# DeltaNet decay rows copied by DMA instead of selector products, and the first loads re-ordered, in a two-layer hybrid trunk

## The chip, the cores and the metric

The kernel runs on one core of one Trainium2 chip. The metric is device time in microseconds (us) of one execution; before the change the median of three runs is 1322.48 us (1322.01 to 1324.29).

## What is computed

Two layers of a decoder trunk run over 272 tokens (16 meta tokens and 256 real ones) with 1024 channels. Each layer is half a SwiGLU feed-forward, a mixer, and half a SwiGLU again, each behind an RMSNorm. The mixer projects the normalised input once and splits it among four branches; the change touches the third, a chunked gated DeltaNet with 4 heads. Cut to what matters:

```
for l in range(DEPTH):
    h = h + 0.5 * swiglu(rmsnorm(h, ln_ffn1[l]), ffn1_wi[l], ffn1_wo[l])
    u = rmsnorm(h, ln_mix[l])
    h = h + hybrid_mixer(u, ...)
    h = h + 0.5 * swiglu(rmsnorm(h, ln_ffn2[l]), ffn2_wi[l], ffn2_wo[l])
y = rmsnorm(h, ln_final)
...
# DeltaNet branch
g = -exp(a_log) * softplus(p_a + dt_bias)
G = cumsum(g)
decay = exp(where(incl, G[:, None] - G[None, :], NEG_INF))
m = eye + where(strict, (kb @ k.T) * decay, 0)
qk = where(incl, (q @ k.T) * decay, 0)
```

So the decays are, for each head, a square over (earlier token, later token): the running sum G of the later token, less that of the earlier one, masked to the causal half, through exp.

## The kernel before, in words

Activations lie transposed, 128 channels to a partition block and 272 tokens along the row. Weights come as fp32 tiles `wf` of up to 1 MB on SyncE's DMA queue; ScalarE (ACT) writes the rounded part `wh` (L210) and VectorE (DVE) the rest `wl` (L184), and TensorE (PE) makes three products `j` for each weight tile, `xh,wh`, `xl,wh` and `xh,wl`. The activations are split likewise into `xh` and `xl`.

The program builds its own order. Every piece of work is a generator with a modelled time (`Chain`), a modelled clock stands for each engine, and a poller emits whichever step the model has ready first; buffers come from small pools ("S" and "L" are row buffers in SBUF, "px" is PSUM). What is emitted is a fixed order for each engine, and each engine runs its own strictly in order. A changed step therefore shifts its neighbours on every engine. Steps on GpSimd (POOL) go through `POOL` (L493), most memsets are emitted where their tile is taken.

The change touches two places. **The head**, `begin` (L729): x comes in four quarters of two tiles `xn`, the meta tokens in `mt`, the first two weight tiles in quarters too, all at once on SyncE's and ACT's queues. `setup` (L464) loads the first norm's gains (`g1r`) and turns them into columns (`g1p`). `columns(q)` transposes a quarter on PE (`xT`), `group(q)` makes `xh`, `xl`, `wh`, `wl` for two k-blocks and the squares for the norm (`scr`), and `before(k)` calls them between the products. **The decays**, `fab` (L1768): the running sums of all heads are three scans into rows 32 to 43 of `pk`, and those of DeltaNet's four heads are rows 36 to 39. Later, for each head, PE spreads one row over all partitions with a selector and adds a mask, and ACT takes the exp from PSUM with the bias `ns` (the earlier token's sum, negated):

```
self.mm(c, ps[:, :T], self.sel[:, h, :], pk[:, :T], True, False)
self.mm(c, ps[:, :T], self.identb, self.maskk, False, True)
```

`setup2` (L559) builds `sel` and `maskk` on POOL and DVE. Behind the running sums, `fab` also sends four rows of the forgetting attention from POOL's queue into `ka`, one for a head.

Of the kernel before, what the change touches and what calls it, by code (L numbers as in the profile page):

```python
# [8 lines left out]
F32 = mybir.dt.float32  # L9
F32R = mybir.dt.float32r  # L10
BF16 = mybir.dt.bfloat16
AF = mybir.ActivationFunctionType
# [3 lines left out]
P = 128  # L16
# [55 lines left out]
class Prog:  # L72
# [391 lines left out]
    def setup(self):  # L464

        nc, i = self.nc, self.i
        c = Chain("setup")
        self.ident = self.const([P, P], F32, "ident")
        self.ones = self.const([P, P], F32, "ones")
        nc.gpsimd.memset(self.ones, 1.0)  # L470
        nc.gpsimd.affine_select(out=self.ident, in_=self.ones, pattern=[[1, P]], compare_op=ALU.is_equal,
                                fill=0.0, base=0, channel_multiplier=-1)
        self.eps = self.const([P, 1], F32, "eps")
        nc.gpsimd.memset(self.eps, EPS)
        self.g1 = self.const([P, L * KD], F32, "g1")
        self.warm(7)
        rows = self.take("S", [L * KD, P], name="g1r")
        nc.scalar.dma_start(out=rows.ap, in_=i["ln_ffn1"].rearrange("l (k p) -> (l k) p", p=P))
        ps = self.take("px", name="g1p")
        c.t = 3500.0  # L480
        self.tr(c, ps[:, :L * KD], rows.ap)
        self.give(rows, c.t)
        self.V(c, "tensor_copy", out=self.g1, in_=ps[:, :L * KD])
        self.give(ps, c.t)
# [74 lines left out]
    def setup2(self, c):  # L559
# [16 lines left out]
        self.maskk = self.const([P, T], BF16, "maskk")  # L576
# [7 lines left out]
        mg = mf  # L584
        yield "pool"
        self.POOL(c, "memset", mg, 0.0)
        yield "pool"
        self.POOL(c, "affine_select", out=mg, in_=mg, pattern=[[1, P]], compare_op=ALU.is_ge,
                                fill=NEG, base=0, channel_multiplier=-1)
        yield "dve"  # L590
        self.V(c, "tensor_copy", out=self.maskk[:, 0:NM], in_=mg[:, 0:NM])
        for b in range(2):
            yield "dve"
            self.V(c, "tensor_copy", out=self.maskk[:, NM + b * P:NM + (b + 1) * P], in_=mg)
# [4 lines left out]
        misc = self.const([P, 768], F32, "sel")  # L599
        sel = misc[:, 0:512].rearrange("p (h c) -> p h c", h=4)  # L600
        o4 = self.ones[:, 0:1].to_broadcast([P, 4 * P]).rearrange("p (h c) -> p h c", h=4)
        yield "pool"
        self.POOL(c, "affine_select", out=sel, in_=o4, pattern=[[-1, 4], [0, P]], compare_op=ALU.is_equal,
                                fill=0.0, base=-36, channel_multiplier=1)
        self.sel = sel
# [22 lines left out]
        sel2 = misc[:, 512:768].rearrange("p (a c) -> p a c", a=2)  # L628
        yield "pool"
        self.POOL(c, "affine_select", out=misc[:, 512:768].rearrange("p (h c) -> p h c", h=4),  # L630
# [98 lines left out]
    def begin(self):  # L729
# [3 lines left out]
        nc.gpsimd.memset(mt.ap, 0.0)  # L733
# [5 lines left out]
        nc.scalar.dma_start(out=mt[0:NM], in_=i["meta"])  # L739
        wfs = [self.wpool.tile([P, 2048], F32, tag=f"wf{x}", name=self.name("wf")) for x in range(2)]  # L740
        for q in range(4):
# [3 lines left out]
            for x in range(2):  # L745
                nc.sync.dma_start(
                    out=wfs[x].rearrange("p (k c) -> p k c", k=KD)[:, 2 * q:2 * q + 2, :],
                    in_=self.chunks[x]["segs"][0][0][2 * q * P:2 * (q + 1) * P].rearrange("(k p) c -> p k c", p=P))
            self.staged[0], self.staged[1] = wfs
        self.nc_ = 2  # L750
        self.tab(AF.Sqrt)
        self.setup()
# [11 lines left out]
        scr = self.take("L", [P, D], name="scr")  # L764

        def columns(q):

            for k in (2 * q, 2 * q + 1):
                c = Chain("x", 3700.0 + 3000 * q)
# [7 lines left out]
        def group(q):  # L777
# [4 lines left out]
            for x, (k, ps, c) in enumerate(now):  # L782
# [6 lines left out]
                wc.t = max(wc.t, 4700.0 + 3000 * q + 1000 * x)  # L789
# [13 lines left out]
            for b in range(2):  # L803
                self.A(Chain("sq"), scr[:, 0:256], xn[b][:, q * 256:q * 256 + 256], AF.Square,
                       accum_out=ss[:, 4 * b + q:4 * b + q + 1])
            if q == 0:
# [4 lines left out]
        def factors(c):  # L811
# [3 lines left out]
            for r in xn + [mt, scr]:  # L815
                self.give(r, self.clk["act"])
# [23 lines left out]
        def before(k):  # L840
# [8 lines left out]
            if k == 3:  # L849
                columns(2)  # L850
                group(2)
            if k == 5:
                columns(3)
                group(3)
                self.LOOK = 0
# [912 lines left out]
    def fab(self, c):  # L1768
# [29 lines left out]
        for a, n in TOK:  # L1798
            yield "dve"
            self.V(c, "tensor_tensor_scan", out=pk[g, a:a + n], data0=self.ones[q, 0:1].to_broadcast([12, n]),  # L1800
                   data1=lg[q, a:a + n], initial=0.0, op0=ALU.mult, op1=ALU.add)
        yield AF.Exp
# [39 lines left out]

        dec = yield from self.take_wait(c, "L", [P, 4, T], name="dec")
        for h in range(4):
            ps = yield from self.take_wait(c, "px", name="dc")
            yield "pe"
            self.mm(c, ps[:, :T], self.sel[:, h, :], pk[:, :T], True, False)
            self.mm(c, ps[:, :T], self.identb, self.maskk, False, True)
            for ti, (a, n) in enumerate(TOK):
                yield AF.Exp  # L1850
                self.A(c, dec[:n, h, a:a + n], ps[:n, a:a + n], AF.Exp,
                       bias=ns[:n, ti * 64 + 16 + h:ti * 64 + 17 + h])
            self.give(ps, c.t)
        for x in st:
            self.give(x, c.t)
        self.dec = dec
# [471 lines left out]
```

## Time and profile before

| | before |
|---|---|
| median of 3 runs, us | 1322.48 |
| the profiled execution, us | 1322.03 |
| its span, us | 1320.3 |
| mean granted TensorE clock | 0.999 |
| PE busy | 99% |
| DVE busy | 66% |
| ACT busy | 54% |
| POOL busy | 15% |
| mean DMA rate | 163 GB/s |

Everything in the span is counted from its start. A timeline row gives the start, the length, the engine and the operation, and in brackets the engine's idle time ahead of it and who ended it. PE's matmuls overlap: a 128x272 product starts about 0.125 us after the one before it although its own row says 0.29, so the cost of a product is read between starts. Layer 0's mixer lies at some 215 to 410 us, layer 1's at some 875 to 1040 us.

### The profile page before, as it was taken

The numbers are of one execution on the slowest core, as the hardware profiler recorded it, in microseconds if no ns is written. First come the engines' busy times: TensorE is split into PE (matmuls) and PEld (weight loads), VectorE is DVE, ScalarE is ACT, GpSimd is POOL, SyncE is SP. The second block draws the span as 40 slices with busy tenths as digits, with TensorE's granted clock in tenths as the row PEclk, the third lists the DMA queues.
The fourth block names the chain that finished last, engine by engine and source line by source line (L and its number), as shares of the span: only waits on it lengthen the run. The fifth ranks groups of instructions, "written<-read, shape, count | busy, mean of one in ns | idle before, by whom it ended". The sixth has DMA issues, their size and how long they took to land.

```text
span 1320.3 us, 25744 instructions
## 1 busy us (share of the span) xinstructions
PE 1301.8 (99%) x10515; PEld 1267.7 (96%) x10515; DVE 876.6 (66%) x1521; ACT 718.5 (54%) x1156; POOL 192.5 (15%) x314
## 2 busy tenths in 40 slices
PE   8999999999999999999999999999999999999998
PEld 8999999999999999999999999999899999999986
DVE  4766556778767876565566565568796778766653
ACT  6445445896544564445454444459865545544542
POOL 1444001100004141110011110011000132111100
PEclk9999999999999999999999999999999999999999
DMA  7656555342333665555555555555333366555561
GB/s 225 195 184 198 176 170 165 111 160 91 118 111 128 202 205 162 190 162 175 176 183 169 182 169 176 172 149 157 100 111 111 117 197 199 192 190 178 197 201 48
DMA packets 210918, 214.62 MB, mean 163 GB/s; under 512 B 13324, under 2 KB 200048, under 8 KB 210800
## 3 DMA queue, kind: packets, MB, share of 16 engines
q1 hardware_dynamic: 208608, 210.62, 49.6%
q0 software_dynamic: 2128, 2.29, 0.7%
q8 instruction: 83, 1.36, 0.4%
q14 instruction: 35, 0.29, 0.1%
q10 hardware_dynamic: 64, 0.07, 0.0%
HBM read 211.90 MB, written 1.05 MB: 161 GB/s over the span
## 4 chain that ended last, share of the span: by engine, by line
PE 86%; ACT 7%; DVE 4%; issue 1%; DMA 1%; POOL 1%; SPq 0%; ACTq 0%; DVEq 0%; POOLq 0%
PE j L235 54%; PE o L235 15%; PE fo L235 5%; PE wo L235 4%; PE br L235 3%; ACT wh L210 2%; ACT L205 2%; DVE wl L184 1%; PE sc L235 1%; PE pv L235 1%; ACT sq L210 1%; DMA wf<-in_ffn_wi_dram 1%; PE pt L247 0%; PE p L235 0%; PE ku L235 0%
## 5 line engine op out<-in xcount | busy, mean ns | idle before, releaser
L235 PE MATMUL j<-xh,wh 128*128 128x272 f32 (+2 forms) x2224 | 647.9, 291 | 0.0
L235 PE MATMUL j<-xh,wl 128*128 128x272 f32 (+2 forms) x2224 | 636.6, 286 | 1.3 <-DVE wl L184 1.3
L235 PE MATMUL j<-xl,wh 128*128 128x272 f32 (+2 forms) x2224 | 635.5, 286 | 0.0
L184 DVE TENSOR_TENSOR wl<-wf,wh 128x1024 fp32r<-128x1024 f32 (+1 forms) x408 | 484.3, 1212 | 183.1 <-ACT wh L210 181.8
L210 ACT ACTIVATE wh<-wf 128x1024 fp32r<-128x1024 f32 (+1 forms) x408 | 408.0, 1027 | 104.4 <-PE o L235 73.0
L235 PEld LDWEIGHTS j<-xh,wh 128*128 128x128 f32 (+1 forms) x2224 | 418.0, 188 | 3.6 <-issue 0.3
L235 PEld LDWEIGHTS j<-xh,wl 128*128 128x128 f32 (+1 forms) x2224 | 418.5, 188 | 2.6 <-DVE wl L184 2.5
L235 PEld LDWEIGHTS j<-xl,wh 128*128 128x128 f32 (+1 forms) x2224 | 418.8, 188 | 0.8
L235 PE MATMUL o<-act,wh 128*128 128x272 f32 x1056 | 199.0, 288 | 0.0
L235 PEld LDWEIGHTS o<-act,wh 128*128 128x128 f32 x1056 | 165.8, 188 | 0.0
L235 PE MATMUL o<-act,wl 128*128 128x272 f32 x528 | 152.2, 288 | 0.0
L197 POOL TENSOR_TENSOR g<-g,R 128x272 f32<-128x272 f32 (+1 forms) x88 | 70.1, 797 | 415.6 <-ACT g L210 415.6
L210 ACT ACTIVATE act<-g 128x272 fp32r<-128x272 f32 (+1 forms) x88 | 37.7, 428 | 133.4 <-DVE g L184 133.4
L210 ACT ACTIVATE g<-g 128x272 f32<-128x272 f32 (+1 forms) x88 | 37.6, 428 | 124.8 <-DVE g L184 124.5
L235 PEld LDWEIGHTS o<-act,wl 128*128 128x128 f32 x528 | 99.4, 188 | 0.0
L184 DVE TENSOR_TENSOR g<-j,g 128x272 f32<-128x272 f32 (+1 forms) x88 | 38.1, 433 | 56.3 <-PE j L235 44.4
L210 ACT ACTIVATE gt<-gt,pv 128x272 f32<-128x272 f32 (+1 forms) x64 | 30.6, 511 | 72.2 <-DVE gt L184 70.9
L184 DVE TENSOR_TENSOR act<-g,act 128x272 fp32r<-128x272 f32 (+1 forms) x88 | 39.2, 446 | 40.4 <-ACT act L210 40.4
L197 POOL TENSOR_TENSOR sq<-sq,sq 128x272 f32<-128x272 f32 (+1 forms) x30 | 24.3, 811 | 240.0 <-ACT sq L210 226.5
L205 ACT ACT_TABLE_LOAD x43 | 55.2, 1283 | 2.9 <-POOL ones L470 2.2
L235 PE MATMUL fo<-wh,act 128*128 128x512 f32 x176 | 55.3, 395 | 0.0
L184 DVE TENSOR_TENSOR g<-j,R 128x272 f32<-128x272 f32 (+1 forms) x88 | 37.9, 432 | 12.1 <-PE j L235 11.7
(356 smaller groups left out, 1330.3 us busy)
## 6 DMA issues: line engine op xcount, KB each, us to landing
wf<-in_ffn_wi_dram SPq DMA_DIRECT2D x86, 1024.0 KB, 5.1
wf<-in_ffn_wo_dram SPq DMA_DIRECT2D x34, 1024.0 KB, 5.1
wf<-in_w_gate_dram SPq DMA_DIRECT2D x32, 1024.0 KB, 5.1
wf<-in_w_in_dram SPq DMA_DIRECT2D x16, 1024.0 KB, 5.2
wf<-in_ffn_wo_dram SPq DMA_DIRECT2D x12, 768.0 KB, 4.5
wf<-in_w_branch_dram SPq DMA_DIRECT2D x16, 512.0 KB, 3.5
wf<-in_w_out_dram SPq DMA_DIRECT2D x8, 1024.0 KB, 5.2
wf<-in_ffn_wi_dram SPq DMA_DIRECT2D x8, 256.0 KB, 4.4
```

The source lines that it names most:

```text
L184: getattr(self.nc.vector, op_)(**kw)
L197: getattr(self.nc.gpsimd, op_)(**kw)
L205: self.nc.scalar.preload_act_table_set(SETS[ok[0]])
L210: self.nc.scalar.activation(out=out, in_=in_, func=func, **kw)
L235: self.nc.tensor.matmul(out, lhsT, rhs, start=start, stop=stop)
```

## The change

In `fab`, right behind the three scans, four DMAs on POOL's queue copy rows 36 to 39 of `pk` (272 numbers, 1088 bytes each) to all 128 partitions of `dec`, one DMA for a head, so 128 pieces of 1088 bytes in each and 512 pieces (557 KB) in a layer. Three affine_selects on POOL then mask `dec` in place, and ACT's exps read and write `dec` in SBUF instead of reading PSUM. The selector, its mask and the PE products for them are gone. In the head, ACT's queue starts with `g1r` and the first quarter of one weight tile, `mt` follows them; the memset of `mt` goes from POOL to DVE, half of the squares from ACT to DVE, and the third and fourth quarter of x are transposed one k-block earlier.

```
@@ fab
+        dec = yield from self.take_wait(c, "L", [P, 4, T], name="dec")
+        d = Chain("dec", c.t)
+        yield "pool"
+        for h in range(4):
+            self.POOL(d, "dma_start", out=dec[:, h, :], in_=pk[36 + h:37 + h, None, :T].to_broadcast([1, P, T]))
+        d.t += 3000
+        for a, n in TOK:
+            self.POOL(d, "affine_select", out=dec[:n, :, a:a + n], in_=dec[:n, :, a:a + n], pattern=[[0, 4], [1, n]],
+                      compare_op=ALU.is_ge, fill=NEG, base=0, channel_multiplier=-1)
+            d.t += 4 * n * 2.0
+        self.dec_t = d.t
...
-        dec = yield from self.take_wait(c, "L", [P, 4, T], name="dec")
-        for h in range(4):
-            ps = yield from self.take_wait(c, "px", name="dc")
-            yield "pe"
-            self.mm(c, ps[:, :T], self.sel[:, h, :], pk[:, :T], True, False)
-            self.mm(c, ps[:, :T], self.identb, self.maskk, False, True)
-            for ti, (a, n) in enumerate(TOK):
-                yield AF.Exp
-                self.A(c, dec[:n, h, a:a + n], ps[:n, a:a + n], AF.Exp,
-                       bias=ns[:n, ti * 64 + 16 + h:ti * 64 + 17 + h])
-            self.give(ps, c.t)
+        c.t = max(c.t, self.dec_t)
+        for ti, (a, n) in enumerate(TOK):
+            for h in range(4):
+                yield AF.Exp
+                self.A(c, dec[:n, h, a:a + n], dec[:n, h, a:a + n], AF.Exp,
+                       bias=ns[:n, ti * 64 + 16 + h:ti * 64 + 17 + h])
@@ begin
-        nc.gpsimd.memset(mt.ap, 0.0)
+        rows = self.take("S", [L * KD, P], name="g1r")
+        nc.scalar.dma_start(out=rows.ap, in_=i["ln_ffn1"].rearrange("l (k p) -> (l k) p", p=P))
+        nc.vector.memset(mt.ap, 0.0)
...
-        nc.scalar.dma_start(out=mt[0:NM], in_=i["meta"])
...
-                nc.sync.dma_start(
+                eng = nc.sync if q or x else nc.scalar
+                eng.dma_start(
...
+            if q == 0:
+                nc.scalar.dma_start(out=mt[0:NM], in_=i["meta"])
...
-            if k == 3:
+            if k == 2:
                 columns(2)
                 group(2)
-            if k == 5:
+            if k == 4:
                 columns(3)
                 group(3)
+            if k == 5:
```

In all, PE loses the 8 `dc` visits (two products each), and ACT's table loads go from 43 to 51: four more among the first layer's setup, two fewer in layer 0's mixer, and six more in layer 1's.

The first place is the head of ACT's order. Before (`mt` meta tokens, `g1r` gains, `xh` and `wh` the split input and weights, `scr` squares):

```order
L739 DMA mt_71<-in_meta_dram 16x1024
L205 ACT_TABLE_LOAD
L478 DMA g1r_132<-in_ln_ffn_dram 16x128
L210 ACTIVATE xh_81<-xT_151,g_9_123 128x272
L210 ACTIVATE wh_137<-wf_98 128x512
L210 ACTIVATE xh_82<-xT_155,g_9_123 128x272
L210 ACTIVATE wh_141<-wf_99 128x512
```

and now:

```order
L714 DMA g1r_72<-in_ln_ffn_dram 16x128
L728 DMA wf_99<-in_ffn_wi_dram 128x2x256
L732 DMA mt_71<-in_meta_dram 16x1024
L205 ACT_TABLE_LOAD
L210 ACTIVATE xh_83<-xT_152,g_10_125 128x272
L210 ACTIVATE wh_137<-wf_99 128x512
L210 ACTIVATE xh_84<-xT_156,g_10_125 128x272
```

`g1r` was issued behind the first table load and is now the first; `mt` stands third instead of first, with a weight quarter ahead of it.

The second place is POOL's order in layer 1's mixer, at the running sums (`gk`, `gq`, `gv`, `lr` are the columns ahead of the convolutions' inputs, `vm` and `vl` the values with their column of ones). Before:

```order
L1366 MEMSET gk_1475_10519 128x3
L1366 MEMSET gq_1479_10556 128x3
L1366 MEMSET gq_1486_10604 128x3
L1366 MEMSET gv_1490_10644 128x3
L1366 MEMSET gv_1509_10732 128x3
L1839 DMA ka_10353<-fab_10455 1x16x17 x4
L1366 MEMSET lr_1533_10907 128x3
```

and now:

```order
L1353 MEMSET gk_1471_10514 128x3
L1353 MEMSET gq_1475_10551 128x3
L492 DMA dec_10579<-fab_10454 128x1x272 x4
L492 AFFINE_SELECT dec_10579<-dec_10579 16x4x16
L492 AFFINE_SELECT dec_10579<-dec_10579 128x4x128 x2
L1353 MEMSET gq_1483_10613 128x3
L1353 MEMSET gv_1487_10653 128x3
L1353 MEMSET gv_1506_10741 128x3
L1838 DMA ka_10348<-fab_10450 1x16x17 x4
```

The copies and selects stand ahead of the second `gq` memset, both `gv` memsets and the `ka` rows, all of which POOL did without them before.

The third place is ACT's order in layer 0's mixer, behind the running sums (`kq` a convolution's first term, `wh` a weight split, `vl` values). Before:

```order
L210 ACTIVATE vm_2890<-vt_2885 128x8x64
L210 ACTIVATE qt_2784<-qr_2809 32x272 x4
L210 ACTIVATE kq_2925<-gk_394_2904,pv_674 128x272
L210 ACTIVATE wh_2932<-wf_2720 128x1024
L210 ACTIVATE dec_2938<-dc_2939,ns_2817 16x16
L210 ACTIVATE vl_2937<-vt_2895 16x64
L210 ACTIVATE dec_2938<-dc_2939,ns_2817 128x128
```

and now:

```order
L210 ACTIVATE vm_2900<-vt_2895 128x8x64
L210 ACTIVATE qt_2781<-qr_2819 32x272 x4
L210 ACTIVATE kq_2935<-gk_395_2914,pv_675 128x272
L210 ACTIVATE wh_2942<-wf_2716 128x1024
L210 ACTIVATE dec_2780<-dec_2780,ns_2827 16x16
L210 ACTIVATE vl_2947<-vt_2905 16x64
```

with, on POOL:

```order
L492 DMA dec_2780<-fab_2683 128x1x272 x4
L492 AFFINE_SELECT dec_2780<-dec_2780 16x4x16
L492 AFFINE_SELECT dec_2780<-dec_2780 128x4x128 x2
L1593 MEMSET vm_2900 128x8
L1353 MEMSET gk_395_2914 128x3
```

ACT's order hardly changes; what moved is the memset of `gk`, which `kq` needs, to behind the copies and the selects, and the exps now read `dec` itself.

## Rows read from the trace of the kernel before

**Rows 1.** the page's busy times, PE

```profile
PE 1301.8 (99%) x10515; PEld 1267.7 (96%) x10515; DVE 876.6 (66%) x1521; ACT 718.5 (54%) x1156; POOL 192.5 (15%) x314
```

**Rows 2.** timeline of PE at the head: start, length, engine, line, operation

```profile
6.89 0.26 PE L247 MATMUL g1p<-ident,g1r 16*128 16x16 f32 x1 [1.58 <-DMA g1r<-in_ln_ffn_dram]
7.08 0.48 PE L247 MATMUL xT<-ident,mt 128*128 128x128 f32 x1
...
9.12 0.57 PE L235 MATMUL j<-xh,wh 128*128 128x272 f32 x1
...
34.49 0.39 PE L235 MATMUL j<-xh,wl 128*128 128x272 f32 x1 [1.04 <-DVE wl L184]
```

**Rows 3.** waits of PE: engine, tile and line, for whom, total us, times, longest

```profile
PE l L235 <- ACT sq L210: 1.4, 3, 0.8
```

**Rows 4.** windows, busy us of each engine (instructions), PEclk, DMA share, GB/s

```profile
890.00:900.00 10.00, 9.52 (x72) 9.07 (x71) 8.73 (x18) 9.81 (x16) 0.00 (x0) 1.00 0.46 132
```

**Rows 5.** timeline of PE, the products around one visit to `dc`, layer 0

```profile
250.00 0.29 PE L235 MATMUL j<-xh,wl 128*128 128x272 f32 x1
...
250.61 0.37 PE L235 MATMUL j<-xh,wh 128*128 128x272 f32 x1
250.82 0.29 PE L235 MATMUL j<-xl,wh 128*128 128x272 f32 x1
```

**Rows 6.** groups by form: xcount, busy us, mean ns, idle before

```profile
L184 DVE TENSOR_TENSOR wl<-wf,wh 128x1024 fp32r<-128x1024 f32 x384 | 466.8, 1241 | 174.2 <-ACT wh L210 173.0
...
L205 ACT ACT_TABLE_LOAD x43 | 55.2, 1283 | 2.9 <-POOL ones L470 2.2
...
L235 PE MATMUL dc<-fab,sel 128*128 128x272 f32 x16 | 5.0, 392 | 0.0
```

**Rows 7.** the tile `mt`: its DMA's duration and start, and time to landing

```profile
L739 ACTq DMA_DIRECT2D mt<-in_meta_dram x1: 390/390/390, 1.8 to 1.8; - x1
...
DMA to landing us min/median/max: 3.8/3.8/3.8
```

**Rows 8.** windows around the loads of `rot`, columns as in rows 4

```profile
86.00:88.40 2.40, 2.40 (x21) 2.40 (x20) 1.54 (x5) 1.80 (x3) 2.32 (x6) 1.00 1.09 380
88.40:89.80 1.40, 1.40 (x13) 1.40 (x12) 1.40 (x2) 0.54 (x1) 0.62 (x1) 1.00 0.88 227
```

**Rows 9.** the DMA view: queues, and issues (KB each, median us to landing)

```profile
q0 software_dynamic: 2128, 2.29, 0.7%
...
rot<-in_rot_dram POOLq DMA_DIRECT2D x4, 68.0 KB, 3.5
```

**Rows 10.** timeline of DVE, the last scan of each layer

```profile
233.89 0.42 DVE L184 TENSOR_TENSOR_SCAN fab<-ones,fab 12x128 f32<-12x128 f32 x1
...
893.73 0.42 DVE L184 TENSOR_TENSOR_SCAN fab<-ones,fab 12x128 f32<-12x128 f32 x1
```

**Rows 11.** the tile `ka`: its uses, and its DMAs' time to landing

```profile
L235 PE MATMUL sc<-ka,qa x40: 180/288/447, 292.2 to 994.0; 65*128 65x144 f32 x16, 65*128 65x272 f32 x16, 65*128 65x16 f32 x8
...
DMA to landing us min/median/max: 1.5/3.0/4.9
```

**Rows 12.** the tile `sel`: its affine_selects, ns min/median/max

```profile
L494 POOL TENSOR_SCALAR_AFFINE_SELECT sel<-ones x2: 416/528/639, 74.0 to 85.8; 128x512 f32<-128x512 f32 x1, 128x256 f32<-128x256 f32 x1
```

**Rows 13.** timeline of POOL, layer 1, memsets of `gq`

```profile
877.39 0.14 POOL L1366 MEMSET gq<- 128x3 f32 x2
```

**Rows 14.** timeline of ACT, layer 1

```profile
899.39 0.51 ACT L210 ACTIVATE kq<-gq,pv 128x272 f32<-128x272 f32 x1
899.80 0.41 ACT L210 ACTIVATE sq<-kq 128x272 f32<-128x272 f32 x1
```

**Rows 15.** timeline of PE, layer 1, the products `l`

```profile
901.83 0.62 PE L235 MATMUL l<-sq,bd 128*128 128x272 f32 x2
```

**Rows 16.** timeline of ACT, layer 0

```profile
245.62 0.52 ACT L210 ACTIVATE kq<-gk,pv 128x272 f32<-128x272 f32 x1
246.05 1.04 ACT L210 ACTIVATE wh<-wf 128x1024 fp32r<-128x1024 f32 x1
```

More of the change, by code (lines that the diff above doesn't have):

```diff
@@ L461, in wtile, with setup @@
         return c
-    def setup(self):
+    def setup(self, rows):
         nc, i = self.nc, self.i
@@ L476, in setup @@
         self.warm(7)
-        rows = self.take("S", [L * KD, P], name="g1r")
-        nc.scalar.dma_start(out=rows.ap, in_=i["ln_ffn1"].rearrange("l (k p) -> (l k) p", p=P))
         ps = self.take("px", name="g1p")
@@ L575, in setup2 @@
         self.maskq = self.const([P, P], BF16, "maskq")
-        self.maskk = self.const([P, T], BF16, "maskk")
         yield "pool"
@@ L583, in setup2 @@
         self.V(c, "tensor_copy", out=self.maskq, in_=mf)
[L584 to L594, printed above, removed]
         st = self.const([P, P], F32, "st")
@@ L598, in setup2 @@
                                 fill=0.0, base=0, channel_multiplier=-1)
[L599 to L605, printed above, removed]
+        misc = self.const([P, 256], F32, "sel")
         e32 = self.const([P, 2, 32], F32, "e32")
@@ L627, in setup2 @@
                    op1=ALU.add)
-        sel2 = misc[:, 512:768].rearrange("p (a c) -> p a c", a=2)
+        sel2 = misc[:, 0:256].rearrange("p (a c) -> p a c", a=2)
         yield "pool"
-        self.POOL(c, "affine_select", out=misc[:, 512:768].rearrange("p (h c) -> p h c", h=4),
+        self.POOL(c, "affine_select", out=misc[:, 0:256].rearrange("p (h c) -> p h c", h=4),
                                 in_=self.ones[:, 0:1].to_broadcast([P, 256]).rearrange("p (h c) -> p h c", h=4),
@@ L751, in begin @@
         self.tab(AF.Sqrt)
-        self.setup()
+        self.setup(rows)
         for b in range(4):
@@ L764, in begin @@
         scr = self.take("L", [P, D], name="scr")
+        scr2 = self.take("S", name="scr2")
         def columns(q):
             for k in (2 * q, 2 * q + 1):
-                c = Chain("x", 3700.0 + 3000 * q)
+                c = Chain("x", 5000.0 + 2600 * q)
                 ps = self.take("px", name="xT")
@@ L788, in group @@
                 src = wfs[x][:, 512 * q:512 * q + 512]
-                wc.t = max(wc.t, 4700.0 + 3000 * q + 1000 * x)
+                wc.t = max(wc.t, 5500.0 + 2600 * q + 500 * x)
                 self.A(wc, hi[:, sl], src, AF.Copy)
@@ L802, in group @@
                 self.give(ps, c.t)
[L803 to L806, printed above, removed]
+            xq = [t[:, q * 256:q * 256 + 256] for t in xn]
+            self.A(Chain("sq"), scr[:, 0:256], xq[0], AF.Square, accum_out=ss[:, q:q + 1])
+            self.V(Chain("sq"), "scalar_tensor_tensor", out=scr2[:, 0:256], in0=xq[1], scalar=1.0, in1=xq[1],
+                   op0=ALU.mult, op1=ALU.mult, accum_out=ss[:, 4 + q:5 + q])
+            if q == 1:
                 self.A(Chain("sq"), scr[0:NM], mt[0:NM], AF.Square, accum_out=ss[0:NM, 8:9])
@@ L814, in factors @@
             dm = self.take("S", [NM, NM], name="dm")
-            for r in xn + [mt, scr]:
-                self.give(r, self.clk["act"])
+            for r in xn + [mt, scr, scr2]:
+                self.give(r, max(self.clk["act"], self.clk["dve"]))
             c.t = self.clk["act"]
```

## The prediction

> **What bounds the kernel now.** I read the page's busy shares first: PE is busy 99% of the 1320.3 us span [rows 1], so what shortens the kernel is a product less, or one of the few stretches in which PE stands. The waits of PE and its timeline give those. At the head PE stands 1.58 us for the gains `g1r` (6.89), starts the transposes at 7.08 and the first product at 9.12, and at 34.49 it stands 1.04 us for a `wl` [rows 2]. In the mixers the products `l` wait 1.4 us for ACT's squares [rows 3]. Then I read who is behind PE in the two mixers: the window of 890 to 900, at layer 1's running sums, shows ACT busy 9.81 of 10 us [rows 4]. What comes late on ACT there reaches PE soon. A 0.2% move, 2.6 us, is about what a measurement of this kernel can tell from no change; I sum against the profiled execution (1322.03), 0.45 us below the median.
>
> **The selector products go.** A visit of PE for one head: the product ahead of it starts at 250.00, the next two products at 250.61 and 250.82; the last pitch holds 0.21 and the others of that stretch 0.125, so 250.00 to 250.82 is 0.82 where two pitches would be 0.25 [rows 5]. That is 0.57 us, eight times 4.6 us. As busy time the selector products have 5.0 us in 16 halves [rows 6], the mask products beside them, overlapped; 4.6 is the time on PE. Nothing hides it, since PE is the bound: **-4.6 us**. The exps stay on ACT, as many and as large, and I cost their new source at nothing.
>
> **The head.** `g1r` was issued behind `mt` and a table load. Now it is first and `mt` third on ACT's queue. An issue takes ACT 0.39 us, so with two ahead of it `mt` is issued at about 1.8, as before, where it took 3.8 us to land [rows 7]: 5.6. So `xT` starts near 5.7 instead of 7.08, 1.4 us earlier, and the first product with it. The stall at 34.49 I expect to go, because DVE's order now has that `wl` ahead of the gating steps it stood behind (1.04 us) [rows 2]. Sum **-2.4 us**; if `mt` lands late it is nothing, if the quarters' small stalls go as well it is -3.5. The memset and the squares now stand on DVE, which is 66% busy over the span [rows 1]; their cover is that nothing of PE waits for DVE ahead of 9.12. The four table loads more in the first layer's setup, 1.283 us each [rows 6], lie on an ACT that is 54% busy [rows 1]; without that room each could cost its length, and I cost them at nothing.
>
> **The copies.** No transfer of the trace reads one partition again and again, so I bound it. Each layer copies 512 pieces of 1088 bytes, 557 KB, all out of four neighbouring partitions. *Lower end*: all 16 engines work side by side, as for weights. The fastest stretch that I read moves 380 GB/s [rows 8]: 1.5 us. *Upper end*: the pieces follow one another at the mean of POOL's own queue, 0.7% of 16 engines' 1320.3 us over 2128 packets, 69 ns [rows 9]: 35 us. *Between*: one after another, at the rate of one engine in that fastest stretch, 380/16 = 23.75 GB/s: 23.5 us. For the slow side speaks the one load into few partitions: `rot`, four times 68 KB into 32 partitions each [rows 9]. While its packets ran, 88.4 to 89.8, the engines were 88% busy and moved 227 GB/s, against 380 just before [rows 8]: with fewer partitions at one end the engines are as busy and move less. Four rows are fewer still, and a single row at a time fewest. I take 23.5 us, the value without any overlap of the reads but at full speed.
>
> [...]
>
> **What waits for them.** POOL's affine_selects wait for all four copies, and POOL runs in order. Layer 1: the last scan starts at 893.73 and ends at 894.15 [rows 10]; the small copies of `ka` on POOL's queue land 3.0 us after issue in the median, 4.9 at worst [rows 11]; with 23.5 us of copying the last lands at 920.7. The selects: a 128x512 select took 0.64 us [rows 12], so two and a small one of about 0.3 make 1.6: 922.2. Only then comes the memset of the second `gq`, which POOL did at 877 before [rows 13]. ACT's `kq` on it ran at 899.39 and its square at 899.80 to 900.21 [rows 14], and PE's `l` on that square started at 901.83 [rows 15]. Now `kq` starts at 922.3, 22.9 us late, the square ends at 923.1, and `l` is 21.3 us late. Behind `kq` on ACT stands the next weight split, so PE finds no other work: its order is fixed. **+21.3 us.** Layer 0: the last scan starts at 233.89 and ends at 234.31 [rows 10]; copies landed 260.8, selects done 262.4. Here the memset of `gk` stands behind them; ACT's `kq` on it ran at 245.62 [rows 16], now 262.5, 16.9 us late. Next on ACT is the split at 246.05 to 247.09 [rows 16]. PE first uses it 24 products behind the visit whose rows I used above [rows 5], at 250.61 + 24 x 0.125 = 253.6 or a little later, and its `wl` at 254.0; `wl`, 1.241 us of DVE [rows 6], was there by 248.3. That is 5.7 us of lead, less the 1.7 us by which three removed visits bring PE forward: 4.0. **+12.9 us**; 16.9 if ACT, packed there too, wins nothing back. The DMAs of `ka` behind the selects come late with them; their first use, by the scores, is at 292 [rows 11], far off.
>
> The sum: -4.6 - 2.4 + 21.3 + 12.9 = +27.2, so 1349.2, with the 0.45 to the median **1349.7 us**.
>
> **The rivals.**
> *A, the copies run side by side: faster.* If the engines overlap the reads, a layer's copies take 1.5 us. In layer 1 the last lands at 898.7 (900.6 at the worst landing), selects done 900.3 to 902.2, `l` 0 to 1.2 us late, say 0.6; in layer 0 the selects are done at 240.4, before 245.62, and nothing is late. -4.6 - 2.4 + 0.6 = -6.4: 1316.1 with the 0.45. It decides wherever the copies take under about 3 us in layer 1 and 12 in layer 0. For it: POOL's queue is nearly idle there, and weights do run on 16 engines at once. Against it: the single source row, and `rot`. [...] The `rot` stretch (88% of 16 engines busy) agrees that the engines take part, not that they get on.
> *B, the copies are quick, and the table loads take the gain.* Layer 1's mixer has six table loads more, 1.283 us each [rows 6], 7.7 us on an ACT that is 98% busy at its start [rows 4]. If all of it reaches PE, A's -6.4 becomes +1.3: 1323.8, no change. Against it: further on in that mixer other steps of ACT wait and may absorb it.
> *C, the reads overlap two by two.* 11.7 us of copying: layer 1 done at 910.5, `l` 9.5 us late; layer 0 done at 250.6, 5.0 late less 4.0 of lead: 1.0. -7.0 + 10.5 = +3.5: 1326.
>
> **How the numbers follow.** My forecast 0.50, A 0.30, B 0.10, C 0.10. C stands just beyond the bound for slower: I count 0.07 of it as slower and 0.03 as the same. So faster 0.30, same 0.13, slower 0.57. The forecast's own range is 1340 to 1362: the cheaper estimate of the copies and more lead below, ACT's full 16.9 and slower pieces above (at 69 ns a piece both layers would add 23 us more, which I leave out). Since A has much of the chance, the range reaches to it: 1314.5 to 1359, which leaves out the lower edge of A and the dearest copies, together under 0.2.
>
> **What would show it.** In the profile after: the landing of `dec`'s DMAs on POOL's queue, some 26 us after issue by my forecast, 4 to 6 by A, 15 by C; their packets' mean length, hundreds of ns against some 50 to 70; POOL's first select in either mixer 26.5 us behind the issue of the copies, or some 5 us; two waits of PE, over 10 us each, in the mixers for ACT, or none; no `dc` group; the first `j` near 7.7 and no wait at 34. More table loads with PE waiting for ACT in small pieces behind 900, and none at the copies, is B. If `dec` lands quickly and there are no long waits, the prediction is wrong at the copies' price; if it lands late and PE goes on, it is wrong at what stands behind them.

## The result, and the profile after

The kernel after takes 1356.09 us (median of 4 runs, 1355.74 to 1356.69) against 1322.24 for the kernel before in the same series: ratio 1.0252, with a 95% interval of 1.0240 to 1.0264. It is 33.9 us slower; the forecast was 1349.7.

The profile's page of the kernel after: the busy times, the granted clock in 40 slices, the queue of POOL's DMAs (packets, MB, share of 16 engines) and the table loads.

```profile
PE 1305.4 (96%) x10491; PEld 1271.8 (94%) x10491; DVE 876.8 (65%) x1527; ACT 727.8 (54%) x1156; POOL 193.4 (14%) x324
...
PEclk9999999899999999999999999997999999999999
...
q0 software_dynamic: 2512, 3.40, 3.5%
...
L205 ACT ACT_TABLE_LOAD x51 | 65.4, 1283 | 3.3 <-DVE mt L715 2.4
```

PE is busy 3.6 us longer than before, in a span of 1355.0 instead of 1320.3 us [rows 1]: it stands some 31 us more. Two slices show a lower clock, the 8th (from 237) and the 28th (from 915): both lie in the mixers. POOL's queue took 0.7% of the DMA engines [rows 9], now 3.5%, for 1.1 MB more. Where PE stands is read from its waits (for whom, total us, times, longest):

```profile
PE l L235 <- ACT sq L210: 21.3, 4, 17.4
PE j L235 <- DVE gk L184: 9.6, 1, 9.6
PE xT L247 <- DMA mt<-in_meta_dram: 2.3, 1, 2.3
PE nrm L235 <- DVE dg L184: 2.0, 1, 2.0
```

The products `l` waited 1.4 us before [rows 3]. The timeline of the kernel after shows the two long waits from their beginning, layer 0 and then layer 1, on DVE, POOL, DVE, ACT and PE:

```profile
235.82 0.42 DVE L184 TENSOR_TENSOR_SCAN fab<-ones,fab 12x128 f32<-12x128 f32 x1
236.84 2.16 POOL L492 DMA_DIRECT2D dec<-fab  x4 [17.18 <-PE qu L235]
259.01 1.42 POOL L492 TENSOR_SCALAR_AFFINE_SELECT dec<-dec 16x64 f32<-16x64 f32 x3 [20.00 <-DMA dec<-fab]
260.43 0.09 POOL L1353 MEMSET gk<- 128x3 f32 x1
260.56 0.52 ACT L210 ACTIVATE kq<-gk,pv 128x272 f32<-128x272 f32 x1 [12.96 <-POOL gk L1353]
263.20 0.43 DVE L184 TENSOR_TENSOR gk<-j,R 128x272 f32<-128x272 f32 x1
263.78 0.56 PE L235 MATMUL j<-xh,wh 128*128 128x272 f32 x1 [9.57 <-DVE gk L184]
...
911.87 0.42 DVE L184 TENSOR_TENSOR_SCAN fab<-ones,fab 12x128 f32<-12x128 f32 x1
912.87 2.18 POOL L492 DMA_DIRECT2D dec<-fab  x4 [17.25 <-PE j L235]
935.14 1.43 POOL L492 TENSOR_SCALAR_AFFINE_SELECT dec<-dec 16x64 f32<-16x64 f32 x3 [20.09 <-DMA dec<-fab]
936.52 0.09 POOL L1353 MEMSET gq<- 128x3 f32 x1
936.65 0.52 ACT L210 ACTIVATE kq<-gq,pv 128x272 f32<-128x272 f32 x1 [19.04 <-POOL gv L1353]
937.54 1.28 PE L235 MATMUL l<-sq,bd 128*128 128x272 f32 x2 [17.43 <-ACT sq L210]
```

POOL issues four copies in 2.2 us and stands 20 us for them. Then come 1.4 us of selects, then a memset of a tenth of a microsecond, and within 0.15 us of that memset ACT starts the `kq` that needed it. PE follows in both layers, by way of ACT's square in layer 1, in layer 0 by way of DVE, whose `gk` (it empties the PSUM buffer that the next `j` needs) stands behind a `kq` and a `wl` that came late. The page's chain of waits names the copies too: in the chain that ended last, the second one is a piece of 20.48 us of `DMA dec<-fab`.

The last scan of each layer cuts the run into three stretches, since everything that the change does to the decays comes behind it. Against 233.89 and 893.73 [rows 10] and the span of 1320.3, the kernel after is at +1.9 at layer 0's scan, gains 16.2 more up to layer 1's, and 16.6 from there to the end. The same three numbers are given below for every kernel run.

### The profile page after: what moved, and what is told of

The parts are those of the page before. It is cut to its first block, busy times and chain, and to the rows that moved or that the text cites. A ratio compares the mean times of both kernels' runs of the same rounds, so it can differ in the third digit from the quotient of the medians.

```text
span 1355.0 us, 25730 instructions
## 1 busy us (share of the span) xinstructions
PE 1305.4 (96%) x10491; PEld 1271.8 (94%) x10491; DVE 876.8 (65%) x1527; ACT 727.8 (54%) x1156; POOL 193.4 (14%) x324
## 4 chain that ended last, share of the span: by engine, by line
PE 84%; ACT 7%; DMA 3%; DVE 3%; issue 2%; POOL 1%; POOLq 0%; ACTq 0%; DVEq 0%
PE j L235 53%; PE o L235 15%; PE fo L235 5%; PE wo L235 3%; PE br L235 3%; DMA dec<-fab 3%; ACT wh L210 2%; ACT L205 2%; PE sc L235 1%; DVE wl L184 1%; PE pv L235 1%; ACT sq L210 1%; ACT gt L210 0%; ACT dec L210 0%; PE pt L247 0%
## 5 line engine op out<-in xcount | busy, mean ns | idle before, releaser
L184 DVE TENSOR_TENSOR g<-j,R 128x272 f32<-128x272 f32 (+1 forms) x88 | 38.0, 432 | 16.4 <-PE j L235 14.9
```

Source lines behind the costliest of these rows:

```text
L184: getattr(self.nc.vector, op_)(**kw)
```

## The experiments

Medians in us; the ratio is to the kernel before on the same chip (1322.24 for the first row, 1322.28 for the next four, 1322.58 for the four after them, 1322.31 for the last three). "To L0", "to L1" and "to the end" are the three stretches of the profiled execution, as us more than before. That is a single execution: that of the last row took 1332.47, 2.0 more than its median.

| kernel | median | ratio, 95% | to L0 | to L1 | to the end |
|---|---|---|---|---|---|
| after | 1356.09 | 1.0252 (1.0240 to 1.0264) | +1.9 | +16.2 | +16.6 |
| decays alone | 1355.96 | 1.0246 (1.0219 to 1.0273) | +0.8 | +16.7 | +16.4 |
| head alone | 1323.21 | 1.0000 (0.9989 to 1.0012) | +1.1 | -0.4 | +0.5 |
| copies out of DRAM | 1328.02 | 1.0037 (1.0025 to 1.0048) | +1.3 | +4.0 | +0.7 |
| memsets on DVE | 1343.52 | 1.0150 (1.0126 to 1.0173) | +1.0 | +16.6 | +3.0 |
| DRAM, weights moved back | 1325.69 | 1.0023 (1.0014 to 1.0032) | +0.5 | +1.8 | +1.5 |
| the same, memsets on DVE | 1321.86 | 0.9995 (0.9986 to 1.0004) | +0.3 | +1.4 | -1.8 |
| copies in two steps | 1336.56 | 1.0104 (1.0090 to 1.0118) | +0.9 | +6.8 | +6.7 |
| head, `mt` first | 1320.46 | 0.9981 (0.9972 to 0.9990) | -2.2 | -0.2 | +0.3 |
| the two mended parts | 1319.17 | 0.9975 (0.9965 to 0.9985) | -3.1 | +1.5 | -1.7 |
| the same, exps later | 1316.43 | 0.9963 (0.9950 to 0.9976) | -2.1 | -2.3 | -1.3 |
| slow copies, hidden | 1330.47 | 1.0061 (1.0048 to 1.0074) | +1.3 | +1.8 | +7.4 |

### The two parts apart

The first kernel has the new `setup2` and `fab` and the old head, the second the new `setup` and `begin` and the old decays. In the first the head is put back:

```diff
@@ begin
-        rows = self.take("S", [L * KD, P], name="g1r")
-        nc.scalar.dma_start(out=rows.ap, in_=i["ln_ffn1"].rearrange("l (k p) -> (l k) p", p=P))
-        nc.vector.memset(mt.ap, 0.0)
+        nc.gpsimd.memset(mt.ap, 0.0)
...
+        nc.scalar.dma_start(out=mt[0:NM], in_=i["meta"])
```

> The decays by DMA, with the head of the kernel before. Theory: the two halves add up, and the new head costs about 2 us (the first down-projection of layer 0 starts 2.06 us later in the changed kernel than in the one before, after a 2.0 us wait of PE at the norm and a stretch of 3 us at half clock). So this is the changed kernel less 2: 1354 us (1352.5 to 1355.5), with PE's waits of some 12 us in layer 0's mixer and some 18 us in layer 1's unchanged. Rival: the head gains the 2.4 us of the prediction, and the mixers lose that much more: 1358 to 1359.

and in the second the decays:

```diff
@@ fab
-            self.POOL(d, "dma_start", out=dec[:, h, :], in_=pk[36 + h:37 + h, None, :T].to_broadcast([1, P, T]))
...
+            self.mm(c, ps[:, :T], self.sel[:, h, :], pk[:, :T], True, False)
+            self.mm(c, ps[:, :T], self.identb, self.maskk, False, True)
```

> The new head, with the selector products of the kernel before. Theory: 1.9 us slower than the kernel before, 1324.1 us (1323 to 1325), with the wait at the norm near 24 and a granted clock below 1.00 for some 3 us behind it. Rival (the prediction's term): 2.4 us faster, 1319.8.

The decays alone give 1355.96, 0.5 above the theory's range and outside the rival's; the head alone gives 1323.21, inside its theory's range, but with a ratio of 1.0000. The whole loss lies in the decays. The head neither gains the forecast's 2.4 us nor loses anything that the times can show; in the stretches it is 1.1 late at layer 0's scan. Why it gains nothing stands in the kernel after. Its tile `mt` first, then PE's timeline at the head:

```profile
L715 DVE MEMSET mt<- x1: 912/912/912, 1.1 to 1.1; 128x1024 f32 x1
L732 ACTq DMA_DIRECT2D mt<-in_meta_dram x1: 335/335/335, 2.0 to 2.0; - x1
...
DMA to landing us min/median/max: 4.8/4.8/4.8
```

```profile
6.96 0.45 PE L247 MATMUL xT<-ident,mt 128*128 128x128 f32 x1 [2.33 <-DMA mt<-in_meta_dram]
...
8.98 0.57 PE L235 MATMUL j<-xh,wh 128*128 128x272 f32 x1
...
24.40 0.69 PE L235 MATMUL nrm<-dg,ones 128*128 128x128 f32 x4 [1.99 <-DVE dg L184]
```

`mt` could be issued only when its memset had ended (1.1 + 0.9), and from 2.0 it took 4.8 us instead of 3.8 [rows 7]. So `xT` starts at 6.96 against 7.08 [rows 2]: one wait was exchanged for another. The quarters, moved up by one k-block, then carry PE to the norm's factors early, and it stands there 2.0 us for DVE.

### Which part of a copy is slow

Two kernels keep the order of every engine (but for the copies themselves) and change only where a copy reads. In the first the four rows go to a DRAM tile, and one DMA spreads them over all partitions from there:

```diff
@@ fab
-        for h in range(4):
-            self.POOL(d, "dma_start", out=dec[:, h, :], in_=pk[36 + h:37 + h, None, :T].to_broadcast([1, P, T]))
+        dr = self.dram.tile([4, T], F32, tag=f"dr{l}", name=self.name("dr"))
+        self.POOL(d, "dma_start", out=dr, in_=pk[36:40, :T])
+        self.POOL(d, "dma_start", out=dec.ap, in_=dr.partition_broadcast(P))
```

> The changed kernel, but the four rows go to DRAM in one small DMA and come back to all 128 partitions in one DMA, on the same queue, the same 557 KB into the same partitions; every other engine's order is the same. Theory (many reads of few neighbouring SBUF partitions are what is slow): the copy is there some 9 us after issue instead of 22 (3 us for the write, 6 for a read as the final gain's copy took before), so nothing waits in layer 0 and PE loses some 3.5 us in layer 1 instead of 18: 1325 us (1321 to 1329). Rival (POOL's queue, or the spreading into 128 partitions in 512 pieces, is slow whatever the source): copies of 18 us or more, 1350 to 1360.

In the second the rows go from their one partition to 32, and three more DMAs take them from those 32 to the rest:

```diff
@@ fab
-            self.POOL(d, "dma_start", out=dec[:, h, :], in_=pk[36 + h:37 + h, None, :T].to_broadcast([1, P, T]))
+            self.POOL(d, "dma_start", out=dec[0:32, h, :], in_=pk[36 + h:37 + h, None, :T].to_broadcast([1, 32, T]))
+        for b in range(1, 4):
+            nc.gpsimd.dma_start(out=dec[32 * b:32 * b + 32, :, :], in_=dec[0:32, :, :])
```

> The changed kernel, but each row is copied to 32 partitions only, and three DMAs copy those 32 partitions to the other 96; all within SBUF, same queue, all other orders the same. Theory (what is slow is many reads out of one partition, or of a few that share a way out): the first stage moves a quarter of the bytes out of one row at a time, 5 us, the second reads 32 partitions and takes 2 to 3 us; with two landings of 3 us the copies are there some 14 us after the first issue instead of 22. Layer 0 loses nothing or 1 us, layer 1 some 8 instead of 18: 1334 us (1329 to 1340). Rival (copies within SBUF are slow whatever they read): second stage 15 us, the whole as long as before or longer, 1355 to 1362.

The tile `dec` in the kernel after: POOL's idle time ahead of the selects (us in both layers, times), and how long its DMAs take from issue to landing.

```profile
  DMA dec<-fab: 40.1, 2
...
DMA to landing us min/median/max: 7.2/14.5/20.5
```

The same out of DRAM:

```profile
  DMA dec<-dr: 6.9, 2
...
DMA to landing us min/median/max: 3.6/4.0/4.3
```

and in two steps:

```profile
  DMA dec<-fab: 10.1, 2
  DMA dec<-dec: 7.4, 2
...
DMA to landing us min/median/max: 3.3/4.3/5.2
```

In the kernel after the four DMAs of a layer land one behind the other, the last 20.5 us after its issue; 557 KB in 20.5 us is 27 GB/s. The same bytes into the same 128 partitions, read out of DRAM, land in 4.0 us. When only a quarter of the bytes comes out of those four partitions, POOL waits 5 us for them in each layer instead of 20, and the three quarters that come out of 32 partitions cost 3.7 us more, landing time included. So it is the reading of few partitions that takes the time, not the writing and not POOL's queue.

Out of DRAM the rows of the four heads also lie end to end, so the pieces could differ as well. The packets say that they do not. Of 2 to 8 KB the page before counts 10752, the kernel after and the one out of DRAM 11008 each: 256 more, so 128 for a layer in both, and 557 KB by 128 is 4352 bytes. The 512 pieces of 1088 bytes of the change's description go four to a packet. POOL's queue in the DMA view (packets with the small ones, MB, share of 16 engines), from 912 to 937 in the kernel after and from 902 to 907 out of DRAM:

```profile
q0 software_dynamic: 192, 0.56, 76.0%
q0 software_dynamic: 144, 0.56, 37.7%
```

A packet takes 1.6 us in the mean in the first (76.0% of 16 times 25 us, by 192) and 0.21 us in the second. And 304 us of packets in some 20 us of copying are about 15 at a time: the engines work side by side, and share 27 GB/s. The times follow: 1328.02, 3 us above its expected point, and 1336.56, both in their expected ranges.

So the copies got 27 GB/s out of their four neighbouring partitions. No run here tells whether that is set by the one partition that a copy reads or by the four together; rows in four distant partitions were not tried.

### What waits behind the copies

Here the copies stay slow, and only the memset of three columns that stood behind them goes to DVE:

```diff
@@ p_evac
-            self.nc.gpsimd.memset(s[:, 0:3], 0.0)
+            self.nc.vector.memset(s[:, 0:3], 0.0)
```

> The changed kernel, but the small memsets ahead of the convolutions' inputs (gk, gq, gv, lr) are made by DVE instead of POOL; the copies and everything else stay. Theory (PE waits because those memsets stand behind the copies on POOL, not because the decays are needed): layer 1's wait of 17.7 us goes, since ACT meets the decays there only later; in layer 0 ACT meets the exps of the decays right behind the next weight split and PE still loses some 5 to 11 of 12 us. 1336 us (1330 to 1342). Rival (the decays themselves are what everything waits for): both waits stay, 1353 to 1357.

1343.52: below the rival's range, but 7.5 us above the theory's point and 1.5 above its range. Layer 1 gives back 13.6 of its 16.6 us, layer 0 nothing. The waits of PE, and then ACT's timeline in both layers, show why:

```profile
PE l L235 <- ACT sq L210: 9.3, 3, 6.7
PE j L235 <- ACT wh L210: 8.5, 1, 8.5
```

```profile
258.40 0.31 ACT L210 ACTIVATE dec<-dec,ns 16x16 f32<-16x16 f32 x1 [10.20 <-POOL dec L492]
...
262.20 1.04 ACT L210 ACTIVATE wh<-wf 128x1024 fp32r<-128x1024 f32 x1
...
937.47 1.06 ACT L210 ACTIVATE wh<-wf 128x1024 fp32r<-128x1024 f32 x1 [5.46 <-DMA wf<-in_w_in_dram]
```

In layer 0 ACT now passes `kq` and one split, but then the first exp waits 10.2 us for the copies, and the `vl` behind it 3.2 us more for a memset that POOL still does behind them; both hold up the weight split that is at 262.20. There the copies have more than one way to PE, and closing one is not enough. In layer 1 what is left is something that no step of the forecast had: a weight load that lands late, because it was issued into the copies (below).

### What the quick copies still cost

The kernel with its copies out of DRAM has short copies and is yet 5.7 us slower than before. Two kernels take that apart. The change makes a constant tile narrower and drops another, and the tiles behind them in SBUF, the weight tiles among them, lie 2592 bytes lower than before; here they are put back, and nothing else is different:

```diff
@@ setup2
-        misc = self.const([P, 256], F32, "sel")
+        misc = self.const([P, 904], F32, "sel")
```

> The kernel with the rows copied by way of DRAM, and one constant tile made wider so that the weight tiles lie at the same SBUF addresses as in the kernel before (without the selector and the mask they lay 2592 bytes lower); no instruction differs. In every kernel with the new decays the products j of the feed-forwards start 126.1 ns apart, in those without 125.3. Theory: it is where the weight tiles lie; the pitch returns to 125.3 and 3 to 4 us come back: 1324.5 us (1323 to 1326). Rival: the pitch is not from the addresses: 1328 as without the wider tile.

and then the memset goes to DVE as well:

```diff
@@ p_evac
-            self.nc.gpsimd.memset(s[:, 0:3], 0.0)
+            self.nc.vector.memset(s[:, 0:3], 0.0)
```

> The same with the wider tile, and the small memsets ahead of the convolutions' inputs made by DVE instead of POOL. Theory: layer 1's wait for the square behind those memsets (1.7 us with the copies by way of DRAM) goes, and nothing else changes: 1322.8 us (1321 to 1325). Rival: PE's waits of that mixer come from ACT being full (six table loads more), so the wait turns up at the next product that needs ACT: as without, 1324.5.

1325.69 and 1321.86, so 2.3 us for the place of the tiles (between chips; by the two ratios it is 1.9) and 3.8 for the memset behind even a short copy: with it on DVE PE's waits for `l` fall from 5.0 to 3.4 us and those for `ns` from 1.9 to 0.5. The first was a surprise. In the first feed-forward, from 60 to 140, PE is without a gap, and the window counts how many products it starts (in brackets). Before, and then with the tiles put back:

```profile
60.00:140.00 80.00, 80.00 (x641) 80.00 (x640) 51.91 (x96) 39.63 (x59) 29.08 (x56) 1.00 0.59 185
60.00:140.00 80.00, 80.00 (x641) 80.00 (x640) 51.49 (x93) 44.64 (x63) 27.01 (x53) 1.00 0.57 184
```

The kernel after has 637 in the same 80 us (its windows stand below), and so has the one out of DRAM, which has the narrow tile too. From 500 to 600 these two and the decays alone start 795 or 796, and the kernel before and all with the old or the wider tile 800 or 801: 0.6% at a granted clock of 1.00 with PE busy throughout. It does not show everywhere (from 160 to 200, in the products `o`, the kernel before, the kernel after and the wider tile all have 321). Which tile's place matters, and why, isn't shown.

### A head that gains

```diff
@@ begin
-        nc.vector.memset(mt.ap, 0.0)
+        nc.scalar.dma_start(out=mt[0:NM], in_=i["meta"])
...
-            if q == 0:
-                nc.scalar.dma_start(out=mt[0:NM], in_=i["meta"])
...
-                self.tr(c, ps[:, 0:P], mt[:, ks])
+                self.tr(c, ps[:, 0:NM], mt[0:NM, ks])
...
-            if k == 5:
+            if k == 6:
```

This is the kernel before with the new head, mended by what the head's rows show: `mt` stands second on ACT's queue and waits for no memset, because only its 16 rows are transposed, and the norm's factors come one k-block later.

> The kernel before with the new head, changed in two points: the meta tokens' 16 rows are transposed alone (no memset of that tile, so its DMA waits for nothing and goes second on ACT's queue), and the norm's factors come one k-block later. Theory (the new head wins 2 us ahead of the norm and loses them there, PE waiting 2.0 us for the factors and then running 3 us at half clock): PE does not wait at the norm, the clock stays at 1.00, the first product comes at 7.3 to 8: 1318.5 us (1317 to 1320.5). Rival: PE is held there by the squares or the weights anyway, and the wait only moves: 1322 to 1324.

1320.46, at the upper end of the theory's range, ratio 0.9981. The timeline of PE now starts the products 1.7 us earlier than before:

```profile
7.40 0.46 PE L235 MATMUL j<-xh,wh 128*128 128x272 f32 x1 [1.47 <-ACT wh L210]
```

What bounds it there is the first weight split, and the wait at the norm's factors is 0.6 us. Most of the forecast's -2.4 for the head was there to be had (-2.2 at layer 0's scan), by an `mt` that lands early and factors that come later, but not with a memset ahead of `mt`.

### Both parts, and the exps moved back

The next kernel is the mended head and the mended decays (copies out of DRAM, tiles put back, memset on DVE) together, the one after it has the exps later in ACT's order as well:

```diff
@@ fab
-        d.t += 3000
+        d.t += 16000
```

This is the modelled time of the copies: a longer one makes the poller emit the exps behind other work.

> The rows by way of DRAM, the wider constant tile and the memsets on DVE, with the mended head (meta tokens alone, the norm one k-block later). Theory (the parts add up): the mixers give 1.1 us net of the removed products (behind the head, the last down-projection came 1.1 us earlier against the kernel before), the head 2.2 to 2.6: 1319 us (1317.5 to 1320.5), less than either alone. Rival: a better head only brings PE sooner to the products that wait for ACT: 1321 to 1322.

> The same, but the planner is told that the rows take 13 us longer than they do, so that ACT's exps of the decays come later; ACT's table loads in the mixers move, in layer 1 from 22 to 17. Theory (what is left of PE's waits for ACT in the mixers comes from exps and table loads put ahead of work that PE needs at the running sums): 1 to 3 us less than the last: 1317 us (1314 to 1319). Rival: the later exps then hold what needs the decays: 1320 to 1324.

1319.17, as the two parts add up (-0.7 and -2.1 against their kernel before), and then 1316.43, ratio 0.9963 with 0.9950 to 0.9976: the fastest of all the kernels here, 5.9 us under the kernel before. Two of its six runs lie at 1320.5 and 1320.9, which makes the interval wide. The table loads on its page:

```profile
L206 ACT ACT_TABLE_LOAD x47 | 60.3, 1283 | 3.0 <-issue 2.2
```

That is four more than before [rows 6]. The timeline of ACT has 17 of them in layer 1's mixer, where the kernel with the two mended parts has 22 and the kernel before 16: of the six more, five are gone. The time is the expected one, but the stretches speak against the loads as its reason: layer 1's stretch is -1.7 with all six, of the -2.3 that its selectors could give, so they had cost it some 0.6, and it is -1.3 without the five. What is gained lies in the stretch of layer 0's mixer, from +1.5 to -2.3. It ends at just the 2.3 us by which four visits of the selector are cheaper. Which of the small waits of that mixer went with the exps' new place wasn't taken apart further; that the first stretch differs by 1.0 with the same head shows how far single executions can be told apart, and the 0.6 is less than that.

### Slow copies that nothing waits for

If the copies cost only by what stands behind them, then they can stay slow. This is the kernel after, head included, with the modelled time of the copies near the measured one, the memsets behind them on DVE, and the tiles put back:

```diff
@@ fab
-        d.t += 3000
+        d.t += 18500
@@ p_evac
-            self.nc.gpsimd.memset(s[:, 0:3], 0.0)
+            self.nc.vector.memset(s[:, 0:3], 0.0)
...
-        self.nc.gpsimd.memset(vm[:, :, :, 64:65], 1.0)
+        self.nc.vector.memset(vm[:, :, :, 64:65], 1.0)
```

> The changed kernel with its slow copies and its head, the wider constant tile, and everything that stood behind the copies moved: the small memsets and those of the values go to DVE, and the planner is told that the copies take 18.5 us instead of 3, so the exps come later. Theory (the copies cost PE only what waits for them, not by their traffic): the copies still take 20 us, no wait of PE over 3 us is left in the mixers: 1322 us (1319 to 1326). Rival (a 20 us transfer out of a few partitions holds up the weights' DMAs or the exps anyway): 1330 to 1345.

1330.47: in the rival's range, not in the theory's. Layer 0 came out (+1.8 instead of +16.2, with the copies as slow as ever), layer 1 did not. ACT's timeline there names the wait, and the DMA view from 896 to 926 its cause (issues, KB each, median us to landing):

```profile
924.20 1.06 ACT L210 ACTIVATE wh<-wf 128x1024 fp32r<-128x1024 f32 x1 [6.70 <-DMA wf<-in_w_in_dram]
```

```profile
wf<-in_w_in_dram SPq DMA_DIRECT2D x3, 1024.0 KB, 16.6
dec<-fab POOLq DMA_DIRECT2D x4, 136.0 KB, 14.9
```

No instruction of ACT or PE waits for the copies any more. But the weights issued while they run take 16.6 us in the median, where the kernel before has 5.2 in that window, and PE stands 7.9 us for `l` behind that split. So the theory is only half right: the copies cost by the order behind them, and where that is mended, by the weights that are issued while they run.

## Why the prediction was right

The prediction was right: slower, because what stands behind slow copies on POOL reaches PE in both mixers. The time lies inside its range, but that says little: 1314.5 to 1359 was drawn so wide that it takes in the rival that was faster. The forecast's own range, 1340 to 1362, holds it too. The sum of +27.2 came out as +34.7 between the two profiled executions, and the terms err in both directions: the copies were cheaper than forecast, and the terms left out cost more than that gave back. By the three stretches:

| stretch | forecast | measured |
|---|---|---|
| to layer 0's last scan (head) | -2.4 | +1.9 |
| to layer 1's (12.9 less 2.3 of selectors) | +10.6 | +16.2 |
| to the end (21.3 less 2.3) | +19.0 | +16.6 |

**The copies: slow as forecast, 4 us too dear in each layer, and near by luck.** The forecast let the first select start 26.5 us behind the issue of the copies. It starts 22.2 and 22.3 us behind (236.84 to 259.01, 912.87 to 935.14), since the reads ran at 27 GB/s, not 23.75. The 23.75 was the rate of one engine, with the pieces one after another; the packets show some 15 under way at once, of 1.6 us in the mean where the forecast looked for hundreds of ns. Nothing in its argument tied what four partitions give to what one engine moves. The lower end of the forecast's range counts on a cheaper estimate of the copies, which no run had shown; what the kernel after showed in its place is the last landing 20.5 us after its issue, where the forecast had 23.5 us of copying and 3.0 of landing. Rival A, and C with it, fell by the 20 us; the `rot` stretch [rows 8] had pointed there, with engines that are busy and move less. In the kernel after it is plainer still. The windows of the kernel after (columns as in rows 4):

```profile
27.00:29.00 2.00, 2.00 (x10) 2.00 (x10) 0.01 (x1) 0.81 (x1) 0.00 (x0) 0.50 1.10 351
60.00:140.00 80.00, 80.00 (x637) 80.00 (x636) 51.39 (x92) 44.20 (x62) 27.09 (x53) 1.00 0.58 184
240.00:259.00 19.00, 14.15 (x112) 13.63 (x110) 6.13 (x15) 5.16 (x8) 0.00 (x0) 0.98 0.93 40
262.00:268.00 6.00, 4.22 (x19) 4.25 (x20) 4.62 (x9) 5.35 (x19) 2.15 (x19) 0.50 0.23 56
938.00:940.00 2.00, 2.00 (x9) 1.77 (x9) 1.90 (x5) 1.95 (x4) 0.00 (x0) 0.50 0.00 0
940.00:941.00 1.00, 1.00 (x6) 0.74 (x6) 1.00 (x4) 0.96 (x3) 0.00 (x0) 0.50 0.00 0
```

From 240 to 259 the DMA engines are 93% busy and move 40 GB/s. For the clock below, a window of the kernel before:

```profile
262.00:268.00 6.00, 5.83 (x45) 5.54 (x44) 5.82 (x10) 5.95 (x10) 0.00 (x0) 1.00 0.53 172
```

**What stands behind them: right in both layers.** Layer 1's `l` starts at 937.54 against 901.83 [rows 15], and 18.1 of that is the delay that it came with (911.87 against 893.73), so 17.6 us are its own, where 21.3 was forecast; the difference is the cheaper copies. PE's longest wait there is 17.4. In layer 0 `kq` starts at 260.56 against 245.62 [rows 16]: less the 1.9 that it came with, 13.0 late, where 16.9 was forecast. PE stands 9.6 us; the lead that it had is then 3.4, the forecast said 4.0. The last link was `gk` on DVE, right behind the `wl` that was forecast, not that `wl` itself. That the memset is what ACT waited for is shown in layer 1 by the run that moves it: 13.6 of the 16.6 us go. In layer 0 moving it is not enough, as the exps and a second memset come in its place; there, with the copies still slow, +16.2 became +1.8 when all of them were moved and the tiles put back.

**Left out: the clock behind a wait.** The term for layer 0, 12.9 for PE's wait, ended with PE's first product. Behind that product, from 262 to 268, the granted clock is 0.50. It had fallen while PE stood (1.00 from 256 to 258, 0.50 from 260 to 262); 19 products start there where the kernel before starts 45. From 268 to 269 it is 0.68, then 1.00: half of the 4.7 us from 263.8 to some 268.5 is lost, 2.3. In layer 1 it is 0.50 from PE's return at 937.5 to 941, so 1.7; with the wait of 17.4 and less the 2.3 of selectors that makes 16.8, where the stretch has 16.6. At the head it is 0.50 from 27 to 29; the wait of 2.0 at the norm's factors had ended at 24.4, and PE had run at 1.00 up to 26. Not each wait brings it: from 275 to 277, behind one of 2.4 us, it is 1.00.

**Left out in layer 0: a second wait, and ACT behind it.** PE stands 2.4 us more for `l` at 273.5. With 9.6, 2.4 and 2.3 less 2.3 for the selectors the stretch has 12.0, and 1.6 more come from the tiles' place (two of the three feed-forwards in which it shows lie here; the decays alone, with the old head, are 0.8 late at the end of the first, and I take that for each). That leaves 2.6 of the 16.2 us that I can't place.

**The head: the failed step.** It said `mt` is "issued at about 1.8, as before, where it took 3.8 us to land", and from that -2.4. It was issued at 2.0 behind its own memset and took 4.8. That the stall at 34.49 would go was right; in its place PE stands 2.0 us for DVE at the norm's factors. The forecast had covered the work moved to DVE only ahead of 9.12 and said nothing of what comes after. Of the stretch's +1.9, 1.1 is in the head alone and 0.8 in the decays alone.

**The selector products: covered; the size fits, but no run takes them away alone.** The fastest kernel has -2.3 and -1.3 in the stretches of the two mixers, most of -4.6. Quick copies alone gave +5.7 (1328.02 less 1322.28) where rival A had -6.4, a gap of 12.1. The runs place 11.2 of it: 2.3 by the tiles' place, 3.8 by the memset, 2.7 by the exps' place on ACT, and 2.4 of head that wasn't gained. Rival B fell, too: its copies were not quick, and the table loads on which it put 7.7 us cost little where they are, since with all six layer 1's stretch is -1.7, and 7.7 more than -2.3 would be +5.4.

## What to carry to other kernels

Price a copy within SBUF by the partitions that it reads, not by its bytes: four rows spread over 128 partitions took 22 us here from the first issue to the first select, and 6 us by way of DRAM. Before an instruction that waits is put on an engine, read what stands behind it in that engine's order, down to a memset of three columns, and what every other engine does with that; then read which transfers will be issued while it waits. And a long wait of PE can cost more than its length: behind those of 9.6 and 17.4 us the first products ran at a granted clock of 0.50.

## What the hardware showed that I had not expected

Weight loads issued into the slow copies were caught in them. On the page of the kernel after, the 512 KB loads take 4.4 us in the median; the one issued in the DMA view from 236 to 262 took 18.9:

```profile
wf<-in_w_in_dram SPq DMA_DIRECT2D x4, 512.0 KB, 4.4
```

```profile
wf<-in_w_in_dram SPq DMA_DIRECT2D x1, 512.0 KB, 18.9
```

In the kernel after this cost nothing, for ACT, which stood for POOL's memset, has no wait for a weight load in its mixers; with the order mended it is what remained, 5.5 us of ACT's waiting with the memsets on DVE and 6.7 with all of it hidden. While the copies run, the 16 DMA engines are 93% busy at 40 GB/s (240 to 259), and in the DMA view from 236 to 262 the packets of POOL's queue take 73.2% of them and those of the weights' queue 6.9%. And 2592 bytes in the place of the tiles made 0.6% in the products of a feed-forward, some 2 us of the whole; what of the place it is stays open.
